# Input projection of both token groups as one seven-product scheme in seven sweeps, with reordered phases and an output projection cut by rows of y

## The chip, the cores and the metric

The kernel runs on one core of a Trainium2 chip. TensorE (PE) multiplies, VectorE (DVE), ScalarE (ACT) and GpSimd (POOL) work elementwise, SyncE (SP) issues all the transfers that this document speaks of, in order, on one queue. The metric is the device time of one execution in microseconds (us). Before the change it was 2970.44 us (median of 3 runs, 2969.25 to 2971.75).

## What is computed

One layer of a hybrid encoder on two groups of tokens with the same weights: G1 with 16 meta tokens and 1024 prompt tokens (1040 columns), G2 with 512 sample tokens (the meta tokens' keys are shared). Width 2048; all data are float32.

```
h = rmsnorm(x, norm_w)                        # (tokens, 2048)
proj = h @ w_in                               # u_f, c_q, c_kv, k_r, q_d, k_d, v_d, gate
y_f  = fft2(u_f).real @ w_fmix                # 4 groups of 128          "f1", "f2"
y_mla = softmax(q k^T) v                      # 8 heads, q, k, v from c_q @ w_uq, c_kv @ w_ukv   "m1", "m2"
y_d  = (softmax(s1) - lam * softmax(s2)) v_d  # 4 heads, bias, rmsnorm   "d1", "d2"
x = x + (concat(y_f, y_mla, y_d) * silu(gate)) @ w_o
out = rmsnorm(x, final_norm)[meta tokens dropped]
```

The input projection has 43 blocks of 128 output columns over 16 blocks of 128 rows; the output projection 16 blocks over 16.

## The kernel before, in words

**Matmuls in three passes.** Every operand is split into a high and a low part that TensorE can take exactly (`split`, L90: a cast on ScalarE, L94, a subtraction on VectorE, L95), and every product is done as high x high, high x low, low x high (`mm`, L337 to 349; `piece`, L313 to 322). A piece of weights is 128 x (4 x 128) elements, 256 KB: it is loaded (tile `wr`), split into `wh` and `wl` and used for four blocks of rows. Three pieces are kept ahead (`fetch_w`, L269, `ahead=3`); `wr`, `wh`, `wl` have three buffers each.

**G1's input projection** (`inproj1`, L351 to 632) uses seven products in place of eight (Strassen's scheme in Winograd's form): the tokens are cut in two halves of 520, the rows of the weights in two halves, and the output blocks are taken in pairs (`PAIRS`, 21 of them, and the single block `kr`). It goes in three waves. Wave 1 does two products with the weights as they are. Beside it, for every pair and half of the rows, a job `s1` loads two pieces into the tile `wq`, adds them (L288) and stores the sum (L289) for later. Wave 2 does two products with weights that the jobs `s23` make from the stored sum (`wq`), one piece in `wr` and one in `wq` (L295, L299). Wave 3 does three products; its jobs `s4` subtract a stored sum (`wq`) from a piece in `wr` (L305). `wq` and `ws` (the sums) have three buffers each (L1415). The partial results go to DRAM and come back (tiles `u`).

**G2's input projection** (`inproj_load`, `inproj`, L634 to 744) is the plain one, eight products' worth, and is done later as filler.

**Order of the work.** PE's order is the program's order; attention and Fourier yield the time that they want filled (`START`, `GAPS`, L1530), and a `Chain` of generators gives that much filler (L1549). After G1's input projection come: `upproj` of G1 (c_q, then c_kv as filler); d1, f1, m1 with G2's input projection as filler; d2 with G2's `upproj`; f2 and m2 with the output projection of G1's first half; then the output projections of G1's second half and of G2, whose last two rows of blocks are cut in two.

**The output projection** (`outproj_load`, `outproj_rows`, `outproj`, `outproj_end`, L1320 to 1382) takes 512 tokens and all 16 blocks of y at once: 48 matmuls per result block, one addition (L1346), then squares and scale; `outproj_end` applies the norm (L1378) and stores to the output (L1381).

Of the kernel before, what the change touches and what calls it, by code (L numbers as in the profile page):

```python
# [17 lines left out]
P = 128  # L18
# [39 lines left out]
HALF = 520  # L58
HK = KD // 2

PAIRS = [(n, b, m) for n, c, m in KINDS if n != "kr" for b in range(0, c, 2)]
_order = lambda *ns: [p for n in ns for p in PAIRS if p[0] == n]
W1 = _order("cq", "ckv", "uf", "kd", "vd", "qd", "gate")
W2 = _order("cq", "ckv", "uf", "kd", "vd", "qd", "gate")
W3 = _order("cq", "qd", "ckv", "uf", "kd", "vd", "gate")
EARLY = 3
G1 = Group(0, 1040, 1024, True, 126, 8, [(0, 0, 346), (512, 346, 346), (1024, 692, 348)], 87, 6, 262, True, 2, 2, 4, 5, 1)
G2 = Group(1, 528, 512, False, 124, 4, [(0, 0, 264), (512, 264, 264)], 89, 3, 264, False, 1, 0, 4, 5, 1)


class K:
# [28 lines left out]
    def rms_cols(self, sp, pp, acc, n, denom, eps):  # L100

        nc = self.nc
        ch = 104 if n % 104 == 0 else 128
# [58 lines left out]
    def scratch(self, dp):  # L162
        for g in (G1, G2):
            s = self.scr[g.i]
            nk = 1040 if g.meta else 512
            for name, c, m in KINDS:
                for b in range(c):
                    s[name, b] = self.t(dp, [P, nk if m else g.nq], f"{name}{b}_{g.i}")
            for h in range(MLA_H):
# [5 lines left out]
            for b in range(16):  # L175
                s["y", b] = self.t(dp, [P, g.nq], f"y{b}_{g.i}")
        self.bvec = self.t(dp, [DIFF_H, NDELTA], "bvec")

        self.ssum = {i: {p[0:2]: self.t(dp, [P, HK, P], f"s{i}{p[0]}{p[1]}") for p in PAIRS} for i in (1, 2)}
        self.part = {(i, *p[0:2]): self.t(dp, [P, HALF], f"u{i}{p[0]}{p[1]}") for p in PAIRS for i in (1, 2, 3)}  # L180
        self.part[1, "kr", 0] = self.t(dp, [P, HALF], "u1kr")
        for n in ("cq", "ckv"):
            self.scr[0]["sq", n] = self.t(dp, [P, HALF], f"sq{n}")
            self.scr[0]["r", n] = self.t(dp, [P, 1040 if n == "ckv" else 1024], f"r{n}_0")


    def w_order(self):
# [6 lines left out]
        def wave1():  # L194
            def s1(p):
                return [("s1", p, q) for q in range(2)]

            def plain(b, qs):
                return [("w", self.ins["win"][b], 4 * q, 4) for q in qs]

            first = [BLOCK0[n] + b for n, b, _ in W1[0:EARLY]]
            for q in (0, 1, 2, 3):
                for b in first:
                    yield from plain(b, (q,))
            for p in W1[0:EARLY]:
                yield from s1(p)
            for i in range(EARLY, len(W1), 2):
                grp = [BLOCK0[n] + b for n, b, _ in W1[i:i + 2]]
                if W1[i][0] == "qd":
                    grp.append(BLOCK0["kr"])  # L210
                for qs in ((0, 1), (2, 3)):
                    for b in grp:
                        yield from plain(b, qs)
                    if qs[0] == 0:
                        for p in W1[i:i + 2]:
                            yield from s1(p)

        def wave2():
            for p in W2:
                for q in range(2):  # L220
                    yield ("s23", p, q)

        def wave3():
            def s(p):
                return [("w", self.ssum[1][p[0:2]], 4 * q, 4) for q in range(2)]

            def a22(p):
                return [("w", self.ins["win"][BLOCK0[p[0]] + p[1] + 1], 8 + 4 * q, 4) for q in range(2)]

            def s4(p):  # L230
                return [("s4", p, q) for q in range(2)]

            for p in W3[0:-2]:
                yield from s(p) + a22(p) + s4(p)
                if p == W3[2]:
                    yield from [("w", self.ins["win"][BLOCK0["kr"]], 4 * q, 4) for q in range(4)]
            for f in (s, a22, s4):
                for p in W3[-2:]:
                    yield from f(p)

        for g in (G1, G2):
            qs = [block("wuq", b, 3, 6) for b in range(12)]
            ups = [p for ps in zip(*qs[0:g.uearly]) for p in ps] + [p for q in qs[g.uearly:] for p in q] + [p for b in range(16) for p in block("wukv", b, 4, 4)]
            if g.meta:
                ins = [*wave1(), *wave2(), *wave3()]
            else:
                first = [block("win", b, 4, KD) for b in range(g.early)]
                ins = [p for ps in zip(*first) for p in ps]
                ins += [p for b in range(g.early, NBLK) for p in block("win", b, 4, KD)]
            out += ins + ups  # L250
        for _ in range(3):
            out += [p for b in range(16) for p in block("wo", b, 4, KD)]
# [16 lines left out]
    def fetch_w(self, ahead=3):  # L269
        nc = self.nc  # L270
        while len(self.w_ready) < ahead and self.w_next < len(self.w_list):
# [7 lines left out]
            kind, (name, b, _), q = job  # L279
            k0 = 4 * q  # L280
            win = self.ins["win"]
            b += BLOCK0[name]
            key = job[1][0:2]
            if kind == "s1":
                a21 = self.raw_w(self.wq, "wq", win[b + 1], k0)
                a22 = self.raw_w(self.wq, "wq", win[b + 1], 8 + k0)
                s1 = self.t(self.wq, [P, 4, P], "ws")
                nc.vector.tensor_tensor(s1, a21, a22, ALU.add)  # L288
                nc.sync.dma_start(self.ssum[1][key][:, k0:k0 + 4, :], s1)  # L289
            elif kind == "s23":  # L290
                s1 = self.raw_w(self.wq, "wq", self.ssum[1][key], k0)
                a11 = self.raw_w(self.wp, "wr", win[b], k0)
                a21 = self.raw_w(self.wq, "wq", win[b + 1], k0)
                s2 = self.t(self.wq, [P, 4, P], "ws")
                nc.vector.tensor_tensor(s2, s1, a11, ALU.subtract)  # L295
                nc.sync.dma_start(self.ssum[2][key][:, k0:k0 + 4, :], s2)
                self.split_w(s2, k0)
                s3 = self.t(self.wq, [P, 4, P], "ws")
                nc.vector.tensor_tensor(s3, a11, a21, ALU.subtract)  # L299
                self.split_w(s3, k0)  # L300
            else:
                a12 = self.raw_w(self.wp, "wr", win[b], 8 + k0)
                s2 = self.raw_w(self.wq, "wq", self.ssum[2][key], k0)
                s4 = self.t(self.wq, [P, 4, P], "ws")
                nc.vector.tensor_tensor(s4, a12, s2, ALU.subtract)  # L305
                self.split_w(s4, k0)
# [30 lines left out]
    def mm(self, w, accs, op, first, last, koff=0, more=False):  # L337

# [3 lines left out]
        for kk in range(n):  # L342
            k = k0 + kk - koff
            for ip, (ww, x) in enumerate(((wh, xh), (wh, xl), (wl, xh))):
                for ps, c, m in accs:
                    self.nc.tensor.matmul(ps, ww[:, kk, :], x[k][:, c:c + m],  # L346
                                          start=(first and kk == 0 and ip == 0), stop=(last and kk == n - 1 and ip == 2),
                                          skip_group_check=more)
            yield 3 * sum(m for _, _, m in accs) / 2400.0

    def inproj1(self, sp, pools, pp):  # L351
# [6 lines left out]
        s = self.scr[0]  # L358
# [10 lines left out]
        def width(m):  # L369
            return HALF if m else 512  # L370

        def accs(m):
            cuts = [(0, 260), (260, 260)] if m else [(0, 512)]
            return [(self.t(pp, [P, 512], "A")[:, 0:w], c, w) for c, w in cuts]

        def xload(k, h):
            xr = self.t(sp, [P, HALF], "xr", bufs=4)
            nc.sync.dma_start(xr, xt[k * P:(k + 1) * P, HALF * h:HALF * h + HALF])
            return xr

# [16 lines left out]
        def load1(k):  # L397
            xr = xload(k, 0)
            operand("b11" if k < HK else "b21", "a" if k < HK else "b", k % HK, xr, g[:, k:k + 1])
            squares(0, xr)  # L400

        def build2(k):
            x12, x22, x11 = xload(k, 1), xload(k + HK, 1), xload(k, 0)
            g1, g2 = g[:, k:k + 1], g[:, k + HK:k + HK + 1]
            squares(1, x12)
            squares(1, x22)
            t = self.t(sp, [P, HALF], "xd", bufs=3)
            nc.scalar.activation(t, x12, AF.Copy, scale=g1)
            t3 = self.t(sp, [P, HALF], "xd", bufs=3)
            nc.vector.scalar_tensor_tensor(t3, x22, g2, t, ALU.mult, ALU.subtract)  # L410
            operand("t3", "d", k, t3)
            t2 = self.t(sp, [P, HALF], "xd", bufs=3)
# [1260 lines left out]
```

## Time and profile before

| | |
|---|---|
| median of the runs | 2970.44 us |
| the profiled execution | 2966.59 us |
| its span, first to last instruction | 2964.7 us |
| mean granted TensorE clock | 0.990 |
| moved by DMA | 510.85 MB in 307638 packets |
| first matmul of what follows G1's input projection | about 904 us |

The page shows each engine's busy time, the span in 40 slices of 74 us, and the costliest groups. "Busy" of PE is the union of the matmuls' spans; these overlap, so a busy PE is not necessarily at its peak. A row of the stage view gives for each engine the busy time within a stretch and, after an x, the number of instructions that touch it; then the granted clock, the mean busy share of the 16 DMA engines and the rate in GB/s.

### The profile page before, as it was taken

What the parts mean: (1) busy time and instruction counts of PE and PEld (TensorE: products, weight loads), DVE (VectorE), ACT (ScalarE), POOL (GpSimd) and SP (SyncE); (2) the same over time, 40 slices, a digit from 0 to 9 for tenths busy, and PEclk for the clock granted to TensorE, in tenths of its full rate; (3) what the DMA queues carried; (4) which work ended last, traced back from release to release, by engine and by line L of the source; (5) the groups of instructions that cost most, each with busy time, mean ns of one, the idle gap of its engine ahead of it and who ended that gap; (6) DMA issues with size and microseconds to landing.
All of it is one profiled execution on the core that took longest, in us unless ns stands there. A gap on an engine that the chain in (4) does not pass through costs nothing.

```text
span 2964.7 us, 45766 instructions
## 1 busy us (share of the span) xinstructions
PE 2866.4 (97%) x16228; PEld 2494.7 (84%) x16228; DVE 1793.7 (61%) x3350; ACT 1258.6 (42%) x2280; POOL 452.8 (15%) x572
## 2 busy tenths in 40 slices
PE   8989999999999999999999999999989999999997
PEld 6877898899987899888888999999878888778787
DVE  6446866655567457778555556565687566553434
ACT  5334322322234456545324444444476455443332
POOL 3111000100001013322102222222012022100101
PEclk9999999999999999999999999999999999999999
DMA  8889988866666455433444333332665543563433
GB/s 277 272 262 311 344 262 261 254 204 207 201 204 215 131 148 160 123 93 114 113 160 140 105 93 90 93 88 74 183 187 174 188 135 118 174 210 118 163 122 121
DMA packets 307638, 510.85 MB, mean 172 GB/s; under 512 B 45024, under 2 KB 100192, under 8 KB 307234
## 3 DMA queue, kind: packets, MB, share of 16 engines
q1 hardware_dynamic: 306960, 504.61, 54.6%
q0 software_dynamic: 448, 3.32, 0.5%
q8 instruction: 128, 2.10, 0.3%
q14 instruction: 102, 0.84, 0.1%
HBM read 385.46 MB, written 122.32 MB: 171 GB/s over the span
## 4 chain that ended last, share of the span: by engine, by line
PE 78%; DMA 9%; DVE 6%; issue 3%; ACT 2%; SPq 1%; POOL 1%; DVEq 0%; ACTq 0%; POOLq 0%
PE A L320 37%; PE A L346 20%; PE S L1063 6%; DMA wq<-in_win_dram 3%; PE T L1217 3%; PE S L1152 2%; PE T L1232 2%; PE T L1233 2%; PE T L1234 2%; DMA xr<-in_xt_dram 1%; DVE wl L95 1%; DMA stage<-y 1%; DVE res L1378 1%; PE S L921 1%; DVE ws L288 1%
## 5 line engine op out<-in xcount | busy, mean ns | idle before, releaser
L94 ACT CAST wh<-wr 128x512 fp32r<-128x512 f32 (+1 forms) x620 | 377.6, 611 | 685.9 <-PE A L320 360.7
L95 DVE TENSOR_TENSOR wl<-wr,wh 128x512 fp32r<-128x512 f32 (+1 forms) x620 | 444.4, 718 | 272.1 <-ACT wh L94 256.6
L320 PE MATMUL A<-yh,wl 128*128 128x512 f32 (+1 forms) x800 | 309.1, 386 | 10.1 <-DVE wl L95 9.9
L320 PE MATMUL A<-yh,wh 128*128 128x512 f32 (+1 forms) x800 | 314.6, 393 | 0.0
L320 PE MATMUL A<-yl,wh 128*128 128x512 f32 (+1 forms) x800 | 307.8, 385 | 0.0
L320 PE MATMUL A<-xh,wh 128*128 128x512 f32 x688 | 286.0, 416 | 0.0
L320 PE MATMUL A<-xh,wl 128*128 128x512 f32 x688 | 271.8, 395 | 3.3 <-DVE wl L95 3.2
L320 PE MATMUL A<-xl,wh 128*128 128x512 f32 x688 | 270.9, 394 | 1.7 <-DVE xl L98 1.7
L320 PEld LDWEIGHTS A<-yh,wl 128*128 128x128 f32 x800 | 151.1, 189 | 44.7 <-DVE wl L95 13.5
L95 DVE TENSOR_TENSOR pl<-T,ph 126x512 fp32r<-126x512 f32 (+1 forms) x240 | 158.0, 685 | 41.1 <-ACT ph L94 39.7
L320 PEld LDWEIGHTS A<-yh,wh 128*128 128x128 f32 x800 | 151.3, 189 | 28.3 <-ACT wh L94 1.7
L320 PEld LDWEIGHTS A<-yl,wh 128*128 128x128 f32 x800 | 151.4, 189 | 25.9
L94 ACT CAST ph<-T 126x512 fp32r<-126x512 f32 (+1 forms) x240 | 131.9, 586 | 93.0 <-PE T L1217 89.3
L94 ACT CAST wh<-ws 128x512 fp32r<-128x512 f32 x126 | 77.8, 619 | 209.3 <-PE A L346 195.0
L1005 DVE CUSTOM_DVE_ANT_1 pe<-S,zero 128x692 f32<-128x692 f32 (+1 forms) x96 | 78.8, 821 | 131.4 <-PE S L1063 131.1
L320 PEld LDWEIGHTS A<-xh,wl 128*128 128x128 f32 x688 | 129.8, 189 | 33.3 <-DVE wl L95 4.1
L346 PE MATMUL A<-xbh,wl 128*128 128x260 f32 (+1 forms) x480 | 141.1, 341 | 12.1 <-DVE wl L95 12.1
L346 PE MATMUL A<-xah,wh 128*128 128x260 f32 (+1 forms) x496 | 142.2, 334 | 8.8 <-ACT xah L97 7.1
L346 PE MATMUL A<-xah,wl 128*128 128x260 f32 (+1 forms) x496 | 142.2, 334 | 7.8 <-DVE wl L95 7.8
L320 PEld LDWEIGHTS A<-xl,wh 128*128 128x128 f32 x688 | 130.9, 190 | 17.3 <-DVE xl L98 2.1
L320 PEld LDWEIGHTS A<-xh,wh 128*128 128x128 f32 x688 | 130.4, 189 | 16.3
L346 PE MATMUL A<-xbh,wh 128*128 128x260 f32 (+1 forms) x480 | 140.7, 340 | 1.8 <-ACT wh L94 1.8
(244 smaller groups left out, 6954.6 us busy)
## 6 DMA issues: line engine op xcount, KB each, us to landing
wr<-in_win_dram SPq DMA_DIRECT2D x390, 256.0 KB, 3.9
wr<-in_wo_dram SPq DMA_DIRECT2D x192, 256.0 KB, 2.8
wq<-in_win_dram SPq DMA_DIRECT2D x126, 256.0 KB, 5.0
xr<-in_xt_dram SPq DMA_DIRECT2D x80, 260.0 KB, 5.3
stage<-in_xt_dram SPq DMA_DIRECT2D x62, 256.0 KB, 2.8
gate<-tmp SPq DMA_DIRECT2D x48, 256.0 KB, 2.9
stage<-y SPq DMA_DIRECT2D x48, 256.0 KB, 3.0
wr<-in_wuq_dram SPq DMA_DIRECT2D x48, 192.0 KB, 2.6
```

The costliest lines, as they stand in the source:

```text
L94: nc.scalar.copy(hi, src)
L95: nc.vector.tensor_tensor(lo, src, hi.bitcast(F32), ALU.subtract)
L288: nc.vector.tensor_tensor(s1, a21, a22, ALU.add)
L320: self.nc.tensor.matmul(ps, ww[:, kk, :], x[k][:, off + c:off + c + m], start=(k == 0 and ip == 0), stop=(k == nk - 1 and ip == 2))
L346: self.nc.tensor.matmul(ps, ww[:, kk, :], x[k][:, c:c + m], start=(first and kk == 0 and ip == 0), stop=(last and kk == n - 1 and ip == 2) ...
L1005: ttr(two(dst), src, two(add), 1.0, -3.0e38, ALU.add, ALU.max, accum_out=mx[0])
L1063: nc.tensor.matmul(ps[:, c:c + n], qq, k[:, k0:k0 + n], start=(ip == 0), stop=(ip == 4))
L1152: nc.tensor.matmul(ps[:, c:c + n], qq[:, sub, sl], ks[sub][:, k0:k0 + n], start=(ip == 0), stop=(ip == 1))
L1217: nc.tensor.transpose(ps[0:g.kc, c, :], pn[0][:, a:a + g.kc], self.ident)
L1232: nc.tensor.matmul(o, vh[:, c, :], ph[:, c, :], start=(c == 0), stop=False)
L1233: nc.tensor.matmul(o, vh[:, c, :], pl[:, c, :], start=False, stop=False)
L1234: nc.tensor.matmul(o, vl[:, c, :], ph[:, c, :], start=False, stop=False)
```

## The change

- Both groups' tokens are projected together. Each half holds 512 prompt, 256 sample and 8 meta tokens (`HALF` 776; `_layout` orders the columns so), and the seven products are done in seven **sweeps**, one product for all 21 pairs after the other (`sweep`). `inproj1`, `inproj_load` and the old `inproj` go. Each accumulator is two PSUM tiles, of 512 and 264 or 256 columns. Two sets of operands of eight tiles remain in place of four; the next one is built while a sweep runs (`t1` ... `b22`).
- The sums of weights are made in the sweep that uses them. The jobs are new; `load` always takes the tile `wq`, whose three buffers stay:

```diff
+            if kind == "a11":
+                a11 = self.raw_w(self.wp, "wr", first, k0)
+                self.split_w(a11, k0)
+                store("s3", add(load(second, k0), a11, ALU.subtract))
+            elif kind == "s1":
+                s1 = add(load(second, k0), load(second, HK + k0), ALU.add)
+                self.split_w(s1, k0)
+                if PAIRS.index(pair) % 2:
+                    store("s1", s1)
+                else:
+                    store("s2", add(s1, load(first, k0), ALU.subtract))
+            elif kind == "s2":
+                s2 = add(load(kept("s1"), k0), load(first, k0), ALU.subtract)
                 self.split_w(s2, k0)
+                store("s2", s2)
+            elif kind == "s3":
+                self.split_w(add(load(second, k0), load(first, k0), ALU.subtract), k0)
             else:
+                self.split_w(add(load(first, HK + k0), load(kept("s2"), k0), ALU.subtract), k0)
```

- The order of the sweeps, by operand, with the weights' jobs and what each does with its product (`keep` stores a partial result, `part` loads one, `result` scales it and stores the projected block to DRAM for both groups):

```
b11  a11 (first 3 pairs plain)           keep p1
t1   s1, 42 jobs                         keep p5
t2   s2 (odd pairs), stored s2 (even)    keep u2 = p1 + product
t3   s3 (first 3 pairs), stored s3       keep u3 = u2 + product; result with p5
t4   plain                               result with u3
b21  plain                               result with p1
b22  s4, 42 jobs                         result with p5 and u2
```

- The phases follow in another order, and the output projection is done in parts by rows of y, with sums kept in DRAM between them:

```diff
+OUT_PARTS = [[(G2, 0, 0, 8), (G2, 0, 8, 8), (G1, 0, 0, 4)],
+             [(G1, 512, 0, 4), (G1, 0, 4, 8), (G1, 512, 4, 8)],
+             [(G1, 0, 12, 4), (G1, 512, 12, 4)]]
...
+            fill = Chain([self.upproj(G2, "cq", uq, sp, pa, tabs), self.upproj(G2, "ckv", uk, sp, pa)])
+            uq, load = self.upproj_load(G1, "cq", xq, sp)
+            fill.merge(load)
+            fill.gens.append(self.upproj(G1, "cq", uq, sp, pa, tabs))
...
+                fill.merge(attend(G2, self.diff_ops, ap, 3))
...
+                fill.merge(self.fourier(G2, ap, pp, START[4], GAPS[4]))
...
+            fill.gens.append(self.upproj(G1, "ckv", uk, sp, pa))
...
+                fill.merge(attend(G2, self.mla_ops, ap, 5))
...
+                fill.merge(self.fourier(G1, ap, pp, START[1], GAPS[1]))
...
+            parts = self.outproj_parts(OUT_PARTS[0], yp, sp, pa)
+            fill = Chain([parts])
...
+                fill.merge(attend(G1, self.mla_ops, ap, 2))
+            fill.gens.append(self.outproj_parts(OUT_PARTS[1], yp, sp, pa))
...
+                fill.merge(attend(G1, self.diff_ops, ap, 0))
+            fill.gens.append(self.outproj_end(G2, 0, (None, fill.values[parts][1]), sp, pa))
+            fill.rest()
...
+            for part in OUT_PARTS[2]:
+                ys.append(([], []))
+                drain(self.y_load(yp, sp, *part, ys[-1]))
+            first, second = OUT_PARTS[2]
+            fill = Chain([self.outproj(first, ys[0], rp, sp, pa)])
+            fill.rest()
+            end = self.outproj_end(G1, 0, fill.value, sp, pa)
```

A part is (group, first token, first block of y, number of blocks). Each of its 16 result blocks loads the sum so far, does 12 or 24 matmuls, adds (VectorE) and stores:

```diff
+            for d in range(16):
+                xr = self.t(sp, [P, 528], "stage", bufs=6)[:, 0:512]
+                self.res_load(xr, g, c0, d, e0 == 0)
+                acc = self.t(pp, [P, 512], "A")
+                for _ in range(0, n, 4):
+                    yield from self.mm(self.next_w(), [(acc, 0, 512)], ys, e0, n)
+                r = self.t(sp, [P, 528], "stage", bufs=6)[:, 0:512]
+                nc.vector.tensor_tensor(r, xr, acc, ALU.add)
...
+                nc.sync.dma_start(self.res[g.i, c0, d], r)
```

The stage tiles of this part of the program, which the loads of y (`y_load`) and the final scaling of G2 (`outproj_end` with `res` None) use as well, have six buffers together. In the last two parts only blocks 12 to 15 of y are left for G1, and the last eight rows of blocks are cut in two halves of 256 tokens, as two were before.

More of the change, by code (lines that the diff above doesn't have):

```diff
@@ L218, in wave2 @@
[L218 to L239, printed above, removed]
@@ new lines, in w_order @@
+        for b in win:
+            out += halves(b + 1, 1)
+        for i, b in enumerate(win):
+            out += halves(b, 1)
+            alone(i, 1)
+        for i, p in enumerate(PAIRS):
+            out += sums("s4", p)
+            alone(i, 1)
+        for _ in (G2, G1):
+            out += [p for b in range(12) for p in block("wuq", b, 3, 6)]
+            out += [p for b in range(16) for p in block("wukv", b, 4, 4)]
+        for _, _, e0, n in [p for parts in OUT_PARTS for p in parts]:
+            out += [("w", self.ins["wo"][b], k0, 4) for b in range(16) for k0 in range(e0, e0 + n, 4)]
@@ L277, in fetch_w @@
                 continue
-            kind, (name, b, _), q = job
+            kind, pair, q = job
+            name, b, _ = pair
             k0 = 4 * q
[L281 to L296, printed above, removed]
+            first, second = self.ins["win"][BLOCK0[name] + b], self.ins["win"][BLOCK0[name] + b + 1]
@@ new lines, in kept, with load, store, add @@
+            def kept(i):
+                return self.sums[i, name, b]
+            def load(src, k):
+                return self.raw_w(self.wq, "wq", src, k)
+            def store(i, sm):
+                nc.sync.dma_start(kept(i)[:, k0:k0 + 4, :], sm)
+            def add(a, c, op):
+                sm = self.t(self.wq, [P, 4, P], "ws")
+                nc.vector.tensor_tensor(sm, a, c, op)
+                return sm
+            if kind == "a11":
[11 more added lines that the diff above has]
+                s2 = add(load(kept("s1"), k0), load(first, k0), ALU.subtract)
@@ L400, in load1 @@
             squares(0, xr)
[L402 to L412, printed above, removed]
-            nc.vector.scalar_tensor_tensor(t2, x11, g1, t3, ALU.mult, ALU.add)
-            operand("t2", "c", k, t2)
@@ L495, in scaled, with part, to, store @@
-        def scaled(lst, h, u=None):
+                st = self.rope(sp, st, n, HALF, tabs)
+            put((name, b), st, h, m)
+        def part(i, p, m):
+            u = self.t(sp, [P, HALF], "u", bufs=6)
+            nc.sync.dma_start(u[:, 0:width(m)], self.part[(i, *p[0:2])][:, 0:width(m)])
+            return u
+        def to(ps_out, lst, u):
+            for ps, c, w in lst:
+                nc.vector.tensor_tensor(ps_out[:, c:c + w], ps, u[:, c:c + w], ALU.add)
+        def store(i, p, m, o):
+            nc.sync.dma_start(self.part[(i, *p[0:2])][:, 0:width(m)], o[:, 0:width(m)])
@@ new lines, in result, with sweep @@
+            finish(p[0], p[1] + o, h, m, st)
+        def sweep(op, koff, kr, evac, build, at=0, hook=None):
+            tiles = list(range(HK))
+            nxt = 0
+            units = []
+            for i, p in enumerate(PAIRS):
+                units.append(p)
+                if i == KR_AT and kr:
+                    units.append(("kr", 0, True))
+            for i, p in enumerate(units[at:]):
+                lst = accs(p[2])
+                for _ in range(2):
+                    w = self.next_w()
+                    yield from self.mm(w, lst, ops[op], HK if w[2] >= HK else 0, HK)
+                evac(p, lst)
+                for d, f in [x for x in later]:
+                    if d == 1:
+                        f()
+                later[:] = [(d - 1, f) for d, f in later if d > 1]
+                if hook:
+                    hook(i)
+                while build and nxt < HK and nxt < (i + 1) * HK / 17:
+                    build(nxt)
+                    nxt += 1
+                if i == 9 and op == "b22":
+                    yield None
+            while build and nxt < HK:
+                build(nxt)
+                nxt += 1
@@ new lines, in inproj @@
+            else:
+                for it, e, p in zip(its, early, PAIRS):
+                    yield from it
+                    keep("p1", p, False, e)
+        hooked = self.bias_vectors(sp, pp)
+        yield from sweep("b11", 0, True, lambda p, lst: keep("p1", p, p[2], lst), t1, EARLY,
+                         lambda i: next(hooked, None) if i > 8 else None)
+        yield from sweep("t1", 0, True, lambda p, lst: keep("p5", p, p[2], lst, part("p1", p, True) if p[0] == "kr" else None),
+                         t2)
@@ new lines, in inproj, with scale, c22 @@
+        yield from sweep("t2", 0, False, lambda p, lst: keep("u2", p, p[2], lst, part("p1", p, p[2])), t3)
+        cols = self.rms_cols(sp, pp, xsq[1], HALF, float(D), 1e-6)
+        done = []
+        def scale(h):
+            if h not in done:
+                self.rms_rows(pp, cols, rbs[h])
+                done.append(h)
+        def c22(p, lst):
+            scale(1)
+            u3 = keep("u3", p, p[2], lst, part("u2", p, p[2]))
+            result(p, 1, 1, p[2], None, u3, part("p5", p, p[2]))
@@ new lines, in inproj, with c21, c12 @@
+        yield from sweep("t3", 0, False, c22, t4)
+        cols = self.rms_cols(sp, pp, xsq[0], HALF, float(D), 1e-6)
+        def c21(p, lst):
+            scale(0)
+            result(p, 1, 0, p[2], lst, part("u3", p, p[2]))
+        yield from sweep("t4", HK, False, c21, b21)
+        yield from sweep("b21", HK, True, lambda p, lst: result(p, 0, 0, p[2], lst, part("p1", p, p[2])), b22)
+        yield None
+        def c12(p, lst):
+            result(p, 0, 1, p[2], lst, part("p5", p, p[2]), None if p[0] == "kr" else part("u2", p, p[2]))
@@ L746, in rope_tab @@
+        yield from sweep("b22", HK, True, c12, None)
     def rope_tab(self, sp, n, pos0):
@@ L1333, in outproj_rows, with y_load, res_load @@
-    def outproj_rows(self, g, c0, loaded, d, res, ssq, cut, ws, sp, pp):
+    def y_load(self, yp, sp, g, c0, e0, n, ys):
+        for e in range(n):
+            raw = self.t(sp, [P, 528], "stage", bufs=6)[:, 0:512]
+            self.nc.sync.dma_start(raw, self.scr[g.i]["y", e0 + e][:, c0:c0 + 512])
+            for tiles, i in zip(ys, "hl"):
+                tiles.append(self.t(yp, [P, 512], f"y{i}{e}", F32R, 2))
+            self.split(ys[0][e], ys[1][e], raw)
+            yield 1.5
+    def res_load(self, dst, g, c0, d, first, cut=(0, 512)):
@@ L1346, in outproj_rows @@
+    def outproj_rows(self, part, ys, d, res, ssq, cut, ws, sp, pp):
+        nc = self.nc
+        g, c0, e0, n = part
+        c, m = cut
+        xr = self.t(sp, [P, 528], "stage", bufs=6)[:, 0:m]
+        self.res_load(xr, g, c0, d, False, cut)
+        acc = self.t(pp, [P, 512], "A")[:, 0:m]
+        if not ws:
+            ws.append(self.next_w())
+        yield from self.mm(ws[0], [(acc, c, m)], ys, e0, n)
+        r = res[d // 2][:, d % 2, c:c + m]
         nc.vector.tensor_tensor(r, xr, acc, ALU.add)
+        self.outproj_scale(d, r, ssq[:, c:c + m], sp)
```

751 lines of the change are left out of this document (263 added, 488 removed).

## Prediction, on record before the result

> **What bounds the kernel now.** I read the page first, then the stage view, then the groups of PE by form, then what the sums of weights wait for.
>
> ```profile
> span 2964.7 us, 45766 instructions
> ...
> PE 2866.4 (97%) x16228; PEld 2494.7 (84%) x16228; DVE 1793.7 (61%) x3350; ACT 1258.6 (42%) x2280; POOL 452.8 (15%) x572
> ...
> PE   8989999999999999999999999999989999999997
> ...
> DMA  8889988866666455433444333332665543563433
> GB/s 277 272 262 311 344 262 261 254 204 207 201 204 215 131 148 160 123 93 114 113 160 140 105 93 90 93 88 74 183 187 174 188 135 118 174 210 118 163 122 121
> ```
>
> PE is busy nearly everywhere, and no other engine is near its limit over the whole span; DMA is close to it in the first ten slices. So the time is PE's work plus what PE loses, and both must be read stage by stage:
>
> ```profile
> core 0: us, PE busy (x) PEld busy (x) DVE busy (x) ACT busy (x) POOL busy (x), PEclk, DMA share, GB/s
> 0.00:50.00 50.00, 37.23 (x133) 26.35 (x134) 38.45 (x44) 30.62 (x52) 22.48 (x21) 0.97 0.89 284
> 50.00:350.00 300.00, 280.24 (x1626) 239.76 (x1625) 177.59 (x272) 116.58 (x213) 34.70 (x22) 0.98 0.90 294
> 350.00:904.00 554.00, 553.40 (x3351) 492.72 (x3349) 329.01 (x533) 154.37 (x249) 23.05 (x19) 1.00 0.75 229
> 1140.00:1200.00 60.00, 55.19 (x334) 50.29 (x333) 44.48 (x90) 36.79 (x71) 27.53 (x24) 0.94 0.50 151
> ```
>
> ```profile
> 2550.00:2965.00 415.00, 389.72 (x1778) 319.33 (x1776) 188.64 (x279) 143.89 (x235) 29.32 (x24) 0.98 0.46 150
> ```
>
> Waves 2 and 3 of G1's input projection (350 to 904 us) lose 0.6 us; wave 1 loses visibly. What does a matmul cost? Two full stretches, one of matmuls of 260 columns and one of 512, and their own lengths:
>
> ```profile
> 375.00:400.00 25.00, 25.00 (x211) 1.00 0.89 273
> 850.00:875.00 25.00, 25.00 (x110) 1.00 0.71 209
> ```
>
> ```profile
> L346 PE MATMUL A<-xcl,wh 128*128 128x512 f32 x208 | 81.8, 393 | 0.0
> L346 PE MATMUL A<-xcl,wh 128*128 128x260 f32 x272 | 54.4, 281 | 0.0
> ```
>
> The count takes every matmul that touches the stretch, so start to start is (25 + 0.393)/110 = 0.231 us for 512 columns and (25 + 0.281)/211 = 0.120 us for 260: 0.45 and 0.46 ns a column. PE pays by columns, with next to nothing per matmul.
>
> Why wave 1 loses:
>
> ```profile
> L288 DVE TENSOR_TENSOR ws<-wq,wq x42: 677/693/1852, 14.8 to 283.8; 128x512 f32<-128x512 f32 x42
> ...
>   DMA wq<-in_win_dram: 69.1, 28
> ```
>
> ```profile
> 80.25 0.33 SPq L289 DMA_DIRECT2D s1ckv<-ws  x1
> 80.63 0.91 SPq L257 DMA_DIRECT2D wq<-in_win_dram  x2
> ...
> 86.59 0.32 SPq L289 DMA_DIRECT2D s1uf<-ws  x1
> 86.96 0.91 SPq L257 DMA_DIRECT2D wq<-in_win_dram  x2
> ```
>
> ```profile
> 85.87 0.69 DVE L288 TENSOR_TENSOR ws<-wq,wq 128x512 f32<-128x512 f32 x1 [3.16 <-DMA wq<-in_win_dram]
> ...
> 92.91 0.69 DVE L288 TENSOR_TENSOR ws<-wq,wq 128x512 f32<-128x512 f32 x1 [4.40 <-DMA wq<-in_win_dram]
> ```
>
> The 42 `s1` jobs form a chain. A job needs two loads into `wq`, which has three buffers; both are freed by the same sum, so the second load of the next job leaves only after it: sum (85.87 to 86.56), store (86.59), loads (86.96), landing, sum (92.91). From the first to the last sum that is (283.8 - 14.8)/41 = 6.56 us a job, over nearly the whole of wave 1. Where the two inputs come through different rings (`wr` and `wq`), jobs with as many `wq` loads keep up with PE:
>
> ```profile
> L295 DVE TENSOR_TENSOR ws<-wq,wr x42: 679/692/695, 297.0 to 526.1; 128x512 f32<-128x512 f32 x42
> ```
>
> (526.1 - 297.0)/41 = 5.59 us a job, which is PE's own pace there (24 matmuls of 512, 24 x 0.231 = 5.54).
>
> **The change part by part.**
>
> *Columns.* Before, G1 has 13 pairs of 512 (7 products x 24 matmuls: 2184), 8 pairs of 2 x 260 with `kr` (2880), and G2 43 x 48 = 2064 of 512: 504.1 + 345.0 + 476.4 = 1325.5 us. After, 21 x 168 + 96 = 3624 of 512, 2184 of 256 and 1440 of 264: 836.4 + 257.7 + 175.2 = 1269.3. That **removes 56 us** of PE's work, all of it from a PE that is busy, so it counts in full. `upproj`, attention and the output projection keep their columns.
>
> *Wave 1.* Of the 904 us of G1's projection 849.1 are columns, 54.9 lost: in the first 50 us some 132 matmuls of 0.231, so 19.5 lost at the start; 0.6 after 350; the other 35 in wave 1. I keep the 19.5 (larger first tiles, fewer of them, same ratio of bytes to columns) and 7 of the 35 for the small matmuls of norms and bias (a guess, inside the range). **28 go.**
>
> *Sweep t1.* Its 42 `s1` jobs now make the weights that PE uses next, so the chain sets PE's pace. A sweep of 22 units is 13 x 24 x (0.231 + 0.118) + 9 x 24 x (0.231 + 0.122) = 185 us of PE, 4.2 us a piece. The chain's price depends on the landing:
>
> ```profile
> wr<-in_wo_dram SPq DMA_DIRECT2D x192, 256.0 KB, 2.8
> wq<-in_win_dram SPq DMA_DIRECT2D x126, 256.0 KB, 5.0
> ...
> stage<-y SPq DMA_DIRECT2D x48, 256.0 KB, 3.0
> ```
>
> 5.0 us at 284 to 294 GB/s, 2.8 for as many bytes at 150 GB/s in the output projection. The sweep moves 51.5 MB (weights 39, p5 9, the next operand 3), 219 GB/s over the 235 us that come out, so 2.8 + 2.2 x 69/143 = 3.9 us (an estimate between the two rows). The chain is then 6.56 - 1.1 = 5.5 us for an odd pair's job; an even pair's has a third load and a second sum on it, 0.42 + 0.69 more, 6.6. 20 x 5.5 + 22 x 6.6 = 254, less three jobs that are made ahead (18), plus the last piece (4): 239, **54 more than 185**. Ends: 11 (landing 2.8) and 98 (landing 5.0).
>
> *Sweep b22.* Its 42 `s4` jobs took one piece through `wr` before; now both come through `wq`, so it is the same chain without the store (0.38): 50 MB, 235 to 240 GB/s, landing 4.2, 6.56 - 0.8 - 0.38 = 5.4 us a job; 39 x 5.4 + 4 = 214, **29 more**. Ends: 0 and 60.
>
> The Trainium skill ("DMA: Bandwidth & Descriptors", Anatomy of one DMA) gives 2.0 us + bytes/436 GB/s for a transfer, measured on GpSimd's path, hence an estimate of 2.6 us for one of 256 KB; the 5.0 and 2.8 us of the rows are both above it. By that price the chain would be 4.2 us, PE's pace, and t1 and b22 would cost 4 and 0.
>
> *Other sweeps.* t2's odd pairs have two such jobs in four pieces, 11 us in 16.8: covered by three pieces ahead. t3's first three pairs have six, some 3 us. I add 5 for VectorE, whose work per unit grows in t3 (additions over 768 columns in place of 512): **8**, ends 0 and 25.
>
> *The phases behind.* Before, 2964.7 - 904 - 476.4 = 1584.3 us without G2's projection. What PE loses there by name:
>
> ```profile
> PE A L320 <- DVE wl L95: 14.7, 4, 5.0
> ...
> PE S L1152 <- DVE sd L1007: 6.3, 11, 1.5
> ```
>
> Two waits of 5 us stand behind the two scalings of G1's output; one stays (-5). The building of G2's operands within d1 (1140 to 1200 us, 4.8 us idle) goes (-5). New: m1 and d1 ask for 196.8 + 239.4 us of filler by `START` and `GAPS`, and the parts give 40 x 16 x 0.64 + 18 = 427.6, so the last 8.6 us of d1 are bare (+8). Then G2's scaling and the last loads of y share six `stage` buffers:
>
> ```profile
> L1378 DVE TENSOR_TENSOR res<-res,rb x44: 411/686/1789, 2586.0 to 2959.1; 128x512 f32<-128x512 f32 x22, 128x256 f32<-128x256 f32 x22
> ...
> L1378 POOL TENSOR_TENSOR res<-res,rb x20: 899/1334/1802, 2586.1 to 2956.7; 128x512 f32<-128x512 f32 x10, 128x256 f32<-128x256 f32 x10
> ```
>
> 16 tiles of 3.0 + 0.7 + 3.0 us (load, factor, store taken as the load) and four loads of y through six buffers: (20 - 6)/6 x 6.7 = 16 us in which PE has nothing. Part can overlap d1's end; I take 10, ends 0 and 16. f1 runs out of filler and m1's start has loads only (+4); in the last parts one addition falls on 12 matmuls in place of 48 (+3). The 80 additional additions (0.69 each) and their loads and stores in m1 and d1 lie beside PE's work; if that cover is gone they cost up to 55. Sum **+15**, ends -10 and +45.
>
> *Sum.* 1269.3 + 19.5 + 7 + 54 + 29 + 8 = 1387 to the end of the sweeps, 1584 + 15 = 1599 behind: span 2986, with the 1.9 us outside it 2988. That is 21 us over the profiled execution's 2966.6; the median of the runs lies 3.9 above that execution, so I say 2992 for the median.
>
> **The rivals.**
>
> *The ring keeps pace (faster).* If landings fall to 2.8 us once the chain is short of work, t1 costs 11 and b22 nothing: 2988 - 43 - 29 - 4 = 2912, on the medians 2916. By the price of the Trainium skill given above it would be some 7 us less. For it: stores and loads are fewer per microsecond than in wave 1, and `s23` jobs kept 5.6 us. Against it: t1 needs 2.5 loads per 4.2 us through three buffers, 5.0 us each from issue to release, of which 0.7 is the sum and 0.4 the issue; and loads leave in pairs. It decides from a landing of about 3.7 us downward, where t1 and b22 together cost 62 and the sum is no change.
>
> *Only t1 is bound (about the same).* b22 has no store between sum and load. Without its 29: 2963 median, within a point of before.
>
> *The chain stays at 6.56 (much slower).* Landings stay at 5.0 us, since each sum releases a burst of loads, stores and partial results at once: +44 in t1, +31 in b22: 3067.
>
> **How the numbers follow.** The forecast (both sweeps bound, landing near 4) 0.46, own range 2965 to 3020; the ring keeps pace 0.25; only t1 0.14; chain as in wave 1 0.15. About 0.2% (6 us) is what a measurement of this kernel can tell from no change. Faster by more: the first rival, most of the second and the forecast's lower tail, 0.38; within it 0.08; slower 0.54. The range goes from just below the first rival to just below the third, 2905 to 3065.
>
> **What would show it.** Right: in the profile after, PE's slices dip in two places only in the first half, between some 7 and 15% of the span (t1) and between 40 and 47% (b22), full in between; sums in these sweeps 5.4 to 6.6 us apart, VectorE idle before them until `wq` lands; t2, t4 and b21 without loss; first matmuls of d2 at about 1390 us; a gap of 10 to 25 us of PE after d1. Wrong: sums 4.2 us apart and PE full in t1 and b22; or a loss of tens of us in m1 and d1, where the parts' additions would then be the cause.

## The result and the profile after

The changed kernel takes **3085.4 us** (median of 4 runs, 3082.1 to 3087.1) against 2969.9 before: ratio 1.039, 95% interval 1.037 to 1.041. It is slower, as forecast, but by 116 us and not by 22, and outside the range. The profiled run spans 3084.4 us. Its page, the lines that answer to those of before:

```profile
span 3084.4 us, 45804 instructions
...
PE 2851.2 (92%) x16360; PEld 2488.6 (81%) x16360; DVE 1813.8 (59%) x3317; ACT 1174.3 (38%) x2130; POOL 435.7 (14%) x546
...
PE   7988889999999999889899999799999989999966
...
PEclk9999999999999999999999999999999989999988
DMA  7677668668775645676656446444433377454375
```

PE is busy 15 us less and the span is 120 us longer. A slice is 77 us. In the sweeps PE's slices fall below nine in the first (the start), in 3 to 6 (154 to 463 us, most of it t1) and in 17 and 18 (1234 to 1388 us, in b22); the deepest are the two sixes at the end. So the two dips that the prediction named as its sign are there, but the second, as will be seen, has another cause than the one it gave. The stage view, one row for each sweep (b11, t1, t2, t3, t4, b21, b22) and one for all that follows:

```profile
core 0: us, PE busy (x) PEld busy (x) DVE busy (x) ACT busy (x) POOL busy (x), PEclk, DMA share, GB/s
7.60:233.50 225.90, 203.40 (x1073) 170.65 (x1074) 117.52 (x120) 76.10 (x134) 44.63 (x20) 0.95 0.71 218
233.50:464.60 231.10, 197.19 (x1059) 165.78 (x1058) 93.95 (x131) 50.66 (x96) 3.84 (x2) 0.97 0.71 221
464.60:651.00 186.40, 180.81 (x1027) 157.43 (x1025) 92.12 (x140) 34.98 (x55) 0.00 (x0) 0.99 0.73 230
651.00:842.30 191.30, 182.75 (x1035) 158.08 (x1034) 109.43 (x146) 46.37 (x70) 26.39 (x14) 0.99 0.78 245
842.30:1028.20 185.90, 180.76 (x1019) 157.71 (x1019) 90.52 (x130) 45.15 (x67) 9.24 (x6) 0.98 0.63 202
1028.20:1235.80 207.60, 196.88 (x1101) 172.41 (x1100) 88.95 (x129) 46.38 (x70) 12.24 (x7) 0.95 0.53 161
1235.80:1452.20 216.40, 197.39 (x1101) 172.29 (x1100) 135.05 (x200) 48.22 (x76) 12.53 (x7) 0.94 0.69 218
1452.20:3084.40 1632.20, 1511.98 (x8966) 1334.20 (x8964) 1084.32 (x2314) 823.37 (x1561) 326.15 (x484) 0.97 0.53 164
```

The sweeps end at 1452 us (forecast 1387), the rest takes 1632 (forecast 1599). Set against the forecast's own terms, with its 185 us for a sweep with `kr` and 176.6 without:

| term | forecast | after |
|---|---|---|
| columns | -56 | -51 |
| start, and b11 beyond 185 | 26.5 | 48.5 |
| t1 beyond 185 | 54 | 46 |
| b22 beyond 185 | 29 | 31 |
| t2, t3, t4, b21 beyond their columns | 8 | 56 |
| all behind the sweeps | 1599 | 1632 |

The -51 is worked out over the whole trace: each matmul at the median start-to-start time of its shape gives 2798 us before and 2747 after. The steps that are more than a tenth longer than the median of their shape exceed it by 166 us in all before and by 333 after; this is called lost time here. The gain of the change is there; 167 us of new losses lie on top of it.

**t1.** VectorE's sums of weights in t1 (what they waited for, then who waited for them), and PE's own waits there:

```profile
L286 DVE TENSOR_TENSOR ws<-wq,wq x41: 678/693/694, 235.6 to 458.8; 128x512 f32<-128x512 f32 x41
...
  DMA wq<-in_win_dram: 107.2, 39
...
  ACT wh L102: 143.3, 32
...
PE A L348 <- DVE wl L103: 24.4, 15, 6.3
PE A L348 <- ACT wh L102: 9.3, 7, 3.3
```

(458.8 - 235.6)/40 = 5.6 us a sum, against a forecast of 5.5 for odd pairs and 6.6 for even ones. By the start times of the sums the step is 5.57 us for odd pairs and 5.58 for even ones: the third load and the second sum of even pairs, for which the forecast added 1.1 us, cost nothing. ScalarE waits 143 us for the sums, and PE 34 us (24.4 + 9.3) for the split weights that are made of them.

**b22** is the surprise. The same view there:

```profile
L286 DVE TENSOR_TENSOR ws<-wq,wq x37: 681/692/695, 1238.3 to 1437.2; 128x512 f32<-128x512 f32 x37
...
  DMA wq<-s2gate: 20.7, 15
...
  ACT wh L102: 3.6, 1
```

Their mean distance, (1437.2 - 1238.3)/36 = 5.5 us, is close to the 5.4 that was forecast, but that is luck: almost nobody waits for these sums, 3.6 us against 143 in t1. The sums keep step with a PE that stands still for something else. What PE waits for in b21 and b22 stands in its list of waits from 1028 to 1452 us:

```profile
PE T L115 <- POOL ssq L454: 29.3, 4, 10.1
```

These are the small matmuls that sum the squares of c_q and c_kv over the features (`rms_cols`). `add_squares` puts them on the list `later` with a 1, so they enter PE's order right after the unit whose squares they need, and PE, in order, waits for the result on VectorE, its square on ScalarE and the addition on GpSimd. It then pays again. The windows around the 10.1 us wait:

```profile
1309.00:1320.00 11.00, 0.88 (x6) 0.56 (x5) 7.36 (x8) 2.32 (x3) 4.06 (x2) 0.64 0.91 269
1320.00:1323.00 3.00, 3.00 (x18) 2.90 (x18) 0.17 (x1) 0.00 (x0) 0.32 (x1) 0.50 0.85 269
1323.00:1326.00 3.00, 3.00 (x12) 2.57 (x12) 0.00 (x0) 0.00 (x0) 1.33 (x1) 0.55 0.87 295
1326.00:1329.00 3.00, 3.00 (x19) 2.64 (x18) 0.35 (x1) 0.62 (x1) 0.00 (x0) 1.00 0.15 55
```

PE is at work again from 1319.6, with a granted clock of 0.50 until about 1325.7. Over the whole trace matmuls at half clock cost some 44 us after and 18 before (their spacing beyond the median of their shape): the price of many holes in place of few. The Trainium skill ("TensorE: Matmul & The Clock Gate", Part 1) says that the clock falls to half after an idle window of about 3.4 us and comes back after as long a time of work; the 6 us at 0.50 here are between one and two such times. In other places of this trace the clock fell after shorter idle times, which the last section lists; there the measurement decides.

**Behind the sweeps.** Three of PE's waits there, the longest of the first at the start of `upproj`, the second at the start of m1, the third where d1 begins:

```profile
PE A L348 <- ACT stage L688: 12.1, 4, 8.3
PE T L854 <- DMA raw<-vm: 11.7, 1, 11.7
PE A L348 <- DVE stage L1235: 7.3, 2, 5.2
```

and those from 2900 us on:

```profile
PE A L348 <- ACT yh L102: 26.5, 2, 23.7
PE A L348 <- DVE res L1257: 11.3, 3, 8.5
```

### The profile page after: what moved, and what is told of

Read it like the earlier page. It is cut to its first block, busy times and chain, and to the rows that moved or that the text cites. A ratio compares the mean times of both kernels' runs of the same rounds, so it can differ in the third digit from the quotient of the medians.

```text
span 3084.4 us, 45804 instructions
## 1 busy us (share of the span) xinstructions
PE 2851.2 (92%) x16360; PEld 2488.6 (81%) x16360; DVE 1813.8 (59%) x3317; ACT 1174.3 (38%) x2130; POOL 435.7 (14%) x546
## 4 chain that ended last, share of the span: by engine, by line
PE 53%; DMA 9%; DVE 7%; issue 5%; ACT 1%; SPq 1%; POOL 1%; DVEq 0%; ACTq 0%; POOLq 0%
PE A L348 33%; PE S L929 6%; PE T L1083 3%; PE S L1018 2%; PE T L1098 2%; DMA wq<-s2gate 2%; PE T L1099 2%; PE T L1100 2%; DMA u<-p5gate 1%; DVE wl L103 1%; DVE ws L286 1%; PE T L115 1%; DMA fu<-uf 1%; DVE st L528 1%; DVE res L1299 1%
## 5 line engine op out<-in xcount | busy, mean ns | idle before, releaser
L348 PE MATMUL A<-x0h,wl 128*128 128x512 f32 x1376 | 360.4, 344 | 29.8 <-DVE wl L103 29.5
L348 PE MATMUL A<-yh,wh 128*128 128x512 f32 (+1 forms) x800 | 329.2, 411 | 45.1 <-ACT yh L102 26.5
L348 PE MATMUL A<-x0h,wh 128*128 128x512 f32 x1376 | 362.2, 345 | 7.6 <-ACT x0h L105 7.6
L348 PE MATMUL A<-x0l,wh 128*128 128x512 f32 x1376 | 359.7, 343 | 0.1
L348 PE MATMUL A<-x1h,wl 128*128 128x512 f32 (+2 forms) x1040 | 273.2, 344 | 32.7 <-DVE wl L103 32.6
L348 PE MATMUL A<-x1h,wh 128*128 128x512 f32 (+2 forms) x1040 | 273.4, 344 | 9.8 <-ACT wh L102 9.7
L348 PE MATMUL A<-x1l,wh 128*128 128x512 f32 (+2 forms) x1040 | 270.4, 341 | 0.0
L348 PEld LDWEIGHTS A<-x0h,wl 128*128 128x128 f32 x1376 | 215.3, 192 | 66.7 <-DVE wl L103 36.1
L348 PEld LDWEIGHTS A<-x0h,wh 128*128 128x128 f32 x1376 | 215.8, 192 | 39.7 <-ACT x0h L105 7.6
L348 PEld LDWEIGHTS A<-x0l,wh 128*128 128x128 f32 x1376 | 216.8, 192 | 32.1 <-DVE x0l L106 0.6
L348 PEld LDWEIGHTS A<-x1l,wh 128*128 128x128 f32 x1040 | 163.1, 191 | 23.7
```

The lines of the kernel that those rows point to most:

```text
L348: self.nc.tensor.matmul(ps, ww[:, kk, :], x[k][:, c:c + m], start=(k == 0 and ip == 0), stop=(k == nk - 1 and ip == 2))
```

## The experiments

**e1, e2, e3: three suspects, one edit each on the changed kernel.** The ring of t1:

```diff
-                s1 = add(load(second, k0), load(second, HK + k0), ALU.add)
+                s1 = add(self.raw_w(self.wp, "wr", second, k0), load(second, HK + k0), ALU.add)
```

> One edit: in the jobs s1 the first of the two pieces goes through the ring wr, which is idle in this sweep; all bytes, sums and stores stay. In the changed kernel sweep t1 took 231 us (233.5 to 464.6) against 185 of matmuls, with sums of a median 5.6 us apart. Theory (the wq ring paces t1): the two inputs no longer share three buffers, sums come at PE's 4.2 us, t1 falls to 190 to 200, the kernel to 3045 to 3060. Rival (DMA throughput or the landing itself paces t1): bytes are the same, so t1 stays within 10 us of 231 and the kernel within 10 us of 3085.

Measured 3053.6 us (-32), ratio to before 1.029 [1.027, 1.031]; t1 is 202.4 us long in place of 231.1, a little over the 190 to 200 expected. The chain through three buffers is real. What it leaves is shown by the sums' waits in e1's t1:

```profile
L286 DVE TENSOR_TENSOR ws<-wr,wq x40: 678/693/696, 230.8 to 418.1; 128x512 f32<-128x512 f32 x40
...
  DMA s2gate<-ws: 39.1, 8
  DMA wq<-in_win_dram: 20.2, 9
```

The small matmuls one unit later:

```diff
-                    later.append((1, lambda: cols.append(self.rms_cols(...))))
+                    later.append((2, lambda: cols.append(self.rms_cols(...))))
...
-                    later.append((2, rows))
+                    later.append((3, rows))
```

> One edit: the small matmuls that sum the squares of c_q and c_kv, and the transposes behind them, come one unit (8.4 us of matmuls) later in PE's order. In the changed kernel PE waits before them four times (5.5, 5.5, 8.7, 10.3 us) and runs at half clock around each. Theory (they stand directly behind the last product of their own sum, whose way over VectorE, ScalarE and GpSimd is longer than nothing): b21 falls from 208 to 188, b22 from 216 to 188 us, the kernel to 3035 to 3050. Rival (b22 is paced by its ring of two loads per job, as the prediction had it): b22 stays above 205 us, because what PE doesn't wait for here it waits for at the weights; the kernel at 3060 to 3070.

Measured 3056.7 (-29), ratio 1.030 [1.028, 1.032]: b21 goes from 207.6 to 189.7, b22 from 216.4 to 205.8. The time lies between the two that were expected, and b22 is on the rival's side of 205; but what PE still waits for there is not the weights (1.0 us), it is one wait of the same kind, of 10.3 us, for which one unit was not enough. The scaling of G2 behind the loads of y, not ahead of them:

```diff
-            fill.gens.append(self.outproj_end(G2, 0, (None, fill.values[parts][1]), sp, pa))
             fill.rest()
+            end = self.outproj_end(G2, 0, (None, fill.values[parts][1]), sp, pa)
...
             fill = Chain([self.outproj(first, ys[0], rp, sp, pa)])
+            fill.merge(end)
             fill.rest()
```

> One edit: the scaling of G2's output (16 tiles through the six stage buffers) moves from between d1 and the last parts to beside the first of the last parts; the loads of y come first. In the changed kernel PE waits 23.9 us there. Theory (the ring of stage tiles is held by the scaling): the wait falls to 5 to 9 us (load of y and split), the kernel to 3060 to 3070. Rival (the last y of d1 itself comes late): the wait stays at 20 us or more and the kernel at 3080 to 3090.

Measured 3061.4 (-24), ratio 1.031 [1.030, 1.033]. The 23.7 us wait is gone from PE's list; the loads of y had stood behind G2's 16 loads through the same six `stage` buffers.

**e4: the three together**, and one input of jobs s2, s3 and s4 through ring `wr` too.

> The three edits together, and the same change of ring in s2, s3 and s4. If the three causes are separate the gains add: some 30 + 45 + 20 us, hence 2980 to 3000, about the kernel before or a little above it. If a shared cause (the rate of the DMA) lies behind them, the gains do not add and the kernel stays above 3020.

Measured 2995.4 (-90), ratio 1.010 [1.008, 1.012]; the single gains add to 85. The sweeps now end at 1384 us, which is where the forecast had them, by luck, since the terms are others.

**e7: the step of the prediction on b22, alone**, on the changed kernel.

```diff
-                self.split_w(add(load(first, HK + k0), load(kept("s2"), k0), ALU.subtract), k0)
+                self.split_w(add(self.raw_w(self.wp, "wr", first, HK + k0), load(kept("s2"), k0), ALU.subtract), k0)
```

> The changed kernel with one edit: in job s4 the load of the input weight goes through ring wr, so that the three buffers of ring wq no longer chain two loads in b22. Theory, from the trace of after: the sums of b22 come every 4.2 us there and keep PE's pace, and its loss lies in the waits at the sums of squares, so b22 stays at 216 within 4 us and the time at 3085 within 5. Rival, which is the step of the prediction: the chain through the ring costs b22 some 29 us, so b22 goes to about 190 and the time to about 3057.

Measured 3071.2, ratio 1.035 [1.033, 1.038], whose interval just overlaps that of the changed kernel. b22 is 214.2 us long in place of 216.4, and PE waits there for the same sums of squares, so the s4 chain was not what it lost. The time is 14 us less, though 5 at most were expected: the profile has 8 us less in t3 and 5 behind the sweeps, where this edit has no instruction; why is open. With the small matmuls one unit later, the ring is worth 4 us in b22 at the most (205.8 in e2, 201.6 in e4).

**e11: more buffers in place of another ring**, on the changed kernel: five in `wq`.

> The changed kernel with one edit: five buffers in ring wq in place of three, all loads through it as before. Theory, that the chain sum, loads, landing, sum through three buffers is what t1 loses: t1 goes from 231 to 198 to 208 us, as in e1, and the time to 3050 to 3062. Rival, that the loads themselves are late, however many buffers stand ready (4 us to land, two in a pair): t1 stays above 220 and the time above 3073.

Measured 3038.6 (-47), ratio 1.024 [1.023, 1.026]. t1 falls to 209.6, just above the range expected, and b11 (220.0) and t2 (178.5) gain as well, which brings the time below its range; b22 stays at 214.3. So the ring is the cause in t1 by two different edits, and in b22 by neither.

**e5: the additions of squares on VectorE.** In e4 the first units still lost 9 us at 24 us, at weights that VectorE splits. VectorE's groups in e4 in the first 30 us:

```profile
L106 DVE SCALAR_TENSOR_TENSOR x0l<-xr,vecs,x0h 128x776 fp32r<-128x776 f32 x8 | 17.5, 2222 | 1.3 <-ACT x0h L105 1.3
L103 DVE TENSOR_TENSOR wl<-wr,wh 128x512 fp32r<-128x512 f32 x3 | 3.4, 1146 | 0.8 <-ACT wh L102 0.8
```

An operation that takes 0.69 us elsewhere takes 1.15 here on the mean. The timeline of e4 shows what goes with it:

```profile
1251.69 1.84 POOL L461 TENSOR_TENSOR ssq<-ssq,tmp 128x776 f32<-128x776 f32 x1 [31.13 <-ACT tmp L449]
...
1252.19 1.90 DVE L103 TENSOR_TENSOR wl<-wr,wh 128x512 fp32r<-128x512 f32 x1
...
1258.73 2.41 POOL L454 TENSOR_TENSOR ssq<-ssq,tmp 128x776 f32<-128x776 f32 x1 [5.19 <-ACT tmp L449]
...
1259.38 2.30 DVE L286 TENSOR_TENSOR ws<-wr,wq 128x512 f32<-128x512 f32 x1
```

Each time GpSimd began first, and VectorE's operation ended some 0.55 us after GpSimd's (1254.09 after 1253.53, 1261.68 after 1261.14): it stood still until the addition was over. So it is with all 26 splits and sums of weights in e4 that began during such an addition: each ended 0.55 us after it. The Trainium skill ("SBUF — State Buffer", Who interferes with whom) states it so: a VectorE instruction with two inputs in SBUF and a GpSimd instruction that reads SBUF lock each other out, and the later one waits for the whole of the other. These rows agree.

```diff
-                nc.gpsimd.tensor_tensor(xsq[h], xsq[h], sq, ALU.add)
+                nc.vector.tensor_tensor(xsq[h], xsq[h], sq, ALU.add)
```

(and the two additions of `add_squares` likewise)

> The kernel with all three edits (e4, 2995 us) with the additions of squares in the sweeps (squares and add_squares) on VectorE in place of GpSimd. Theory, that VectorE's operations run 1.1 to 1.6 us longer while GpSimd adds (0.69 becomes 2.30, 0.68 becomes 1.90 in e4): the wait of 9.3 us at 24 us shrinks to under 3, b11 goes from 221.7 to 208 to 216, and the time to 2975 to 2985. Rival, that VectorE's own work is what PE waits for at the start: some 50 additions of 0.8 us more on it (40 us) leave b11 as long or longer, and the time is 2995 to 3010.

Measured 2969.2 (-26 from e4), ratio 1.001 [1.000, 1.003]. The same groups in e5:

```profile
L106 DVE SCALAR_TENSOR_TENSOR x0l<-xr,vecs,x0h 128x776 fp32r<-128x776 f32 x8 | 8.2, 1025 | 1.2 <-ACT x0h L105 1.1
L398 DVE TENSOR_TENSOR ssq<-ssq,tmp 128x776 f32<-128x776 f32 x8 | 7.7, 962 | 0.0
```

With eight additions more VectorE spends 15.9 us where it spent 17.5. PE's wait is 2.2 us in place of 9.2, b11 210.7 us in place of 221.7, t1 197.4 in place of 205.5. That is more than the 10 to 20 expected. The e4 profile is of a run 11 us above e4's median, so the totals of the two traces say too much: the seven sweeps are 22 us shorter in e5, and the rest, where this edit has no instruction, is 17 us shorter too, which it doesn't explain.

**e6: sweep b11 with its weights as they are**, s3 made in t3 for all pairs.

```diff
             if i >= EARLY:
-                out += sums("a11", p)
+                out += halves(BLOCK0[p[0]] + p[1], 0)
...
-            out += sums("s3", p) if i < EARLY else [("w", self.sums["s3", *p[0:2]], k0, 4) for k0 in (0, 4)]
+            out += sums("s3", p)
```

> e4 with sweep b11 loading its weights as they are (no second load, no subtraction, no store of s3), and with s3 made in t3 for all pairs from two loads, as now for the first three. Theory, that the 20 us that b11 loses past its first units come from its a11 jobs (two loads and a store for each piece): b11 goes from 221.7 to about 205, t3 from 192.7 to 190 to 198, and the time to 2978 to 2988. Rival, that they come from the slowed VectorE and not from the jobs: b11 stays within 4 us, t3 becomes 5 to 10 longer for its 36 sums more, and the time is 2995 to 3005.

Measured 2960.7 (-35 from e4), ratio 0.998 [0.997, 1.000]. b11 goes to 204.1, and t3 does not pay for it: 184.7 in place of 192.7, though it has 36 sums more. Its weights no longer come back from a store, but that this is the reason was not tried, and t4, where the edit has no instruction, is 6 us shorter too. The wait at the start, which has no such jobs, stays.

**e8: e5 and e6 together**, the small matmuls one unit later still, and the scaling of the output (`eng` in `outproj_end`) on VectorE alone.

> e4 with the edits of e5 and e6, the small matmuls of the sums of squares one unit later still, and the scaling of the last rows on VectorE alone (GpSimd took each third). Theory, that all these are separate waits: e5 gives 10 to 20, e6 7 to 17, the later matmuls the 9 us wait at 1252, the scaling 3 to 6 of the 8.7 us wait at 2939, together 30 to 50, and the time is 2945 to 2965, at or below that of the kernel before. Rival, that VectorE becomes the bound when it has GpSimd's additions and 36 sums more: 2975 to 3000.

Measured **2927.4 us, ratio to before 0.986 [0.984, 0.989]**: faster than both kernels, than the one before by 1.4%, and better than the 2945 to 2965 expected. Its stage view, b11, t1, b21, b22 and the rest:

```profile
7.50:204.40 196.90, 194.22 (x1072) 165.95 (x1073) 88.25 (x110) 76.33 (x134) 0.00 (x0) 0.99 0.53 163
204.40:403.70 199.30, 188.06 (x1059) 162.38 (x1058) 89.81 (x131) 51.23 (x96) 0.00 (x0) 1.00 0.77 250
...
943.50:1133.20 189.70, 189.70 (x1100) 166.43 (x1099) 91.86 (x137) 46.46 (x70) 3.61 (x2) 1.00 0.60 185
1133.20:1323.00 189.80, 189.80 (x1101) 166.52 (x1100) 137.39 (x205) 48.16 (x76) 5.47 (x2) 1.00 0.79 252
1323.00:2926.80 1603.80, 1507.64 (x8966) 1328.85 (x8964) 1081.46 (x2334) 823.18 (x1561) 302.30 (x464) 0.98 0.53 167
```

In b21 and b22 PE has no idle time left. Lost time over the whole trace is 178 us, of which half clock some 14: 12 more than before (166), so most of the columns' gain comes out at last (38 us against the runs of before taken beside it).

**e9, e10, e12: three tries for the rest**, each on e8: five buffers for the sums (`ws`); the stores of the Fourier blocks from GpSimd's queue; five buffers in `wq`.

> e8 with five buffers for the sums of weights (ws) in place of three. Theory, that the 14 us which t1 still loses in e8 come from sums that wait until the store of an earlier sum has landed and frees its buffer (41.9 us of VectorE's waits there name s2gate<-ws): t1 goes from 199.3 to 186 to 192 us and the time to 2914 to 2921. Rival, that the landing of the two inputs is as late and takes the place of that wait: t1 stays at 196 to 200 and the time at 2924 to 2930.

> e8 with the stores of the Fourier blocks (y<-fyt) issued from GpSimd's queue in place of SyncE's. Theory, that m1's first loads stand behind the last of these stores in SyncE's queue: the wait of 10.7 us between f1 and m1 falls to 3 to 7, and the time by 4 to 8, to 2920. Rival, that the loads wait for the memory that f1 gives back at its end: the wait and the time stay within 2.

> e8 with five buffers in ring wq in place of three. Theory, that part of the 14 us that t1 still loses in e8 is the same ring (one input still comes through it, two for even pairs), since e11 gained more in t1, b11 and t2 than e1's ring wr did in t1 and t2: t1 goes from 199.3 to 188 to 195 us and the time to 2912 to 2922. Rival, that with one load through each ring three buffers are enough, and that the rest of t1 is the landing itself: t1 stays at 194 to 201 and the time at 2924 to 2933.

Measured 2932.8, ratio 0.989 [0.988, 0.991]; 2931.7, 0.989 [0.987, 0.990]; 2930.6, 0.988 [0.986, 0.990]. None can be told from e8, so none of the three gains that were expected came. In e9 t1 stays (200.9), and the waits named s2gate<-ws stay at 37.6 us though buffers are free, so the buffers are not what they show; what holds t1's last 11 us is open. In e10 PE's waits between f1 and m1 change name only, from e8:

```profile
PE T L854 <- DMA raw<-vm: 10.6, 1, 10.6
```

to e10:

```profile
PE A L348 <- DVE yl L103: 6.8, 2, 4.3
PE S L929 <- ACT kh L102: 2.4, 1, 2.4
```

and m1 begins 19.3 us after f1's last matmul, 18.3 in e8: the loads of m1 come, and then the loads of y are late. In e12 t1 is 195.0, 4 us shorter; but it is 194.4 in e10, whose edit has nothing to do with t1, so this is no more than two traces differ.

## Why the prediction was wrong

*Direction.* Slower was right, but in part by luck. Without the 29 us for b22, which the ring did not cost, the forecast's sum is the second rival's: no change. Of the losses t1's was forecast; most of the rest lies in terms that it had at 8 and 15 us, or that it kept from the kernel before.

*Columns, -56.* Right in the main: -51. In e8, with 12 us more of lost time than before, 38 of them show in the time.

*Wave 1, 28 go.* Wrong. Start and b11 lose 48.5 us. I kept the loss at the start by "same ratio of bytes to columns" and counted no cost for the jobs that make s3 on the way. Both terms were shown: GpSimd's additions of squares, now 776 wide and beside VectorE's first splits (e5: 11 us of b11), and the a11 jobs (e6: 18 us of b11); in e8, with both edits, b11 is 25 us shorter than in e4.

*t1, +54.* Right in mechanism and nearly in size: 5.6 us a sum against a forecast of 5.5 and 6.6, +46; e1 and e11 show the cause. The 1.1 us more for even pairs was wrong. What e1 and e11 leave, 17 and 25 us beyond 185, only partly yields to rings.

*b22, +29.* The size came out (31) and the mechanism is wrong: e7 and e11 leave b22 as it is, e2 takes 11 us off it, and in e8, with the small matmuls one unit later still, it is at 189.8 (202.6 in e5 and 203.6 in e6, where a wait of some 10 us remained). I carried t1's chain over without looking at what differs: a job of s4 has two loads and one sum, and nobody waited for them.

*Other sweeps, +8.* The largest miss: 56, of which b21 alone is 23. The step that failed there and in b22 is "7 of the 35 for the small matmuls of norms and bias (a guess...)": it priced matmuls, and the cost was the wait in PE's order for the result, the square and the addition, four times, with the half clock after each. The list `later` and its 1 stood in the diff. What would have shown it is asking, for each instruction on the engine with a fixed order, which chain must end before it. The other 33 us are 10 in t2, 15 in t3 and 9 in t4. "Covered by three pieces ahead" failed in t2: five buffers (e11) take 8 us off it. For t3 and t4 no single edit shows the cause.

*The phases behind, +15.* It was +48 (1632 against 1584), the second largest miss. "16 us in which PE has nothing... I take 10" was a wait of 23.7, worth 24 (e3): the loads of y stood behind all 16 tiles of G2's scaling and not among them. "f1 runs out of filler and m1's start has loads only (+4)" was a wait of 11.7. Not in the forecast at all: 8.3 us at the start of `upproj`, where G1's loads of c_q take the `stage` buffers that its results need (read from the trace, not tried). The one wait behind a scaling that the forecast kept, of 5 us, was 8.5. Of the 80 further additions in m1 and d1 two held PE up where d1 begins, for 7.3 us, one of them because its sum landed late; in m1 they lay beside PE's work as forecast (from 1960 to 2490 us PE is idle for 3).

*The rivals.* The first (the ring keeps pace) is false for t1. The second (only t1 is bound) has the ring right, t1 bound and b22 not, and the time wrong, 2963. The last (landings stay at 5.0 us) has the nearest time, 3067, by a cause that isn't there: t1's loads landed in 4.1 us at the median. No rival had many small waits of PE, each with its half clock, as the way to lose.

## What to carry to other kernels

Where one engine's order is written by hand and it is the bottleneck, go through every instruction of it that isn't bulk work, and put it a unit or more behind the last step of the chain that it needs; price the wait and the slow clock after it, not the instruction. When a plan saves work and comes out slower, compare lost time and work apart, sweep by sweep: here 51 us were won and 167 lost, and each of five small edits gave back 24 to 35. Three buffers that both inputs of one operation share come free together, so its loads leave in pairs behind it; a second ring or two more buffers took 29 and 21 of the 46 us that this cost in t1.

## What the runs showed of the hardware

An addition of 128 x 776 on GpSimd took 1.8 to 2.5 us, and VectorE's splits and sums of weights, with two inputs in SBUF, that began during one stood still until it was over: 0.69 us became up to 2.4. The same additions on VectorE took 0.96 us. Here the work on the less busy engine was dearer than on the busier one. The clock fell to half after idle times of PE shorter than 3 us too: in the changed kernel after 2.69, 2.99 and 1.96 us (at 154, 178 and 215 us), each followed within 1.1 us by a stretch at half clock that the records give as 3.41 us. The length of the idle time doesn't decide it alone: after 3.34 us (at 303 us of the same trace) the clock stayed at 1.00.
